# Layer 1 of a two-layer sequence mixer on one core: gates before cells, and five pairs of projections by seven block products

## The chip, the cores and the metric

One core of one Trainium2 chip runs the whole program. Its engines are TensorE (PE, matmuls, with PEld for its weight loads), VectorE (DVE), ScalarE (ACT), GpSimd (POOL) and SyncE (SP, which issues DMAs here). The metric is device microseconds (us) of one execution; lower is better.

## The reference, cut to what matters

x is [512 tokens, 2048] in float32. Layer 0 is an attention layer, which the change leaves as it is. Layer 1 is an mLSTM layer:

```python
proj = x @ w_in                                   # 2048 -> q 1024, k 1024, v 2048, o 2048, gates 16, z 2048
qk = silu(causal_conv4(qk)); q, k = split(qk)     # 8 heads of 128
cell = mlstm(q, k, v, gates)                      # 8 heads of 256, decays from the gates
cell = rmsnorm(cell) * head_norm                  # per head
y = (sigmoid(o) * cell * silu(z)) @ w_out
out = layernorm(ALPHA * x + y)
```

Everything is float32, and the result has to keep close to float32's accuracy.

## The kernel before

**How a product is made.** PE multiplies float32r, a float32 of shorter mantissa. `split` (L166) therefore writes a number as high half plus low half: ACT copies it, rounded, into `hi` (L168), and DVE subtracts to get `lo` (L169). `mm3` (L199) takes three matmuls for a product: hi by hi, hi by lo, lo by hi. The activations of layer 1 (`x1`, 16 k tiles of [128, 512 tokens]) stay in SBUF as pairs. The weights come from HBM in units of 128 partitions by 1024 values: `weights` (L172) loads a unit on SP's queue into one of three `raw` buffers (L181), and `split` turns it into one of three `whi` and three `wlo` buffers.

**Two forms of GEMM.** `gemm_b` (L205) gives [128 columns, 512 tokens] tiles with the weights stationary; a unit is 4 k tiles of 256 columns, 24 matmuls. `gemm_a` (L221) gives [128 tokens, 512 columns] tiles with the activations stationary; a unit is 2 k tiles of 512 columns, 24 matmuls for four token blocks and 12 for two. PSUM has four banks under the name `acc` for these and four under `ps` for everything else.

**Layer 1** is `mlstm` (L798). For each of four pairs of heads it runs a GEMM for the values of both heads (`v_block`, L787), the gate o and z of the first (`gate_out`, L694: two `gemm_b`, Sigmoid on ACT, two multiplies, the last on POOL at L709), q and k of both heads with the causal convolution and SiLU (`conv_silu`, L682), and then o and z of the second head. Each head's cell is a task (`cell`, L725): four steps of q by k with the decays (`decays`, L718, loads them over POOL's queue; L733 is the exponential, L739 the product), then for each of four token blocks the values, a normaliser, a root mean square (L755 to L764, with POOL's power at L255 and a Newton step at L260 to L263), transposes on PE and a multiply into the gate's tile (L773). Values of the first pair are made in two calls, since the second two token blocks of x1 are still being turned when they begin (`Turned`, L846). The gate rows (`gates` and `gate_rows`, L615 and L634) are a task too: a short GEMM and some thirty operations of 8 partitions on DVE.

**What sets the order.** Tasks are generators. `tick` (L116), called between matmuls of a GEMM, runs the next step of a task when a clock that counts matmul columns has come as far as the step's last `yield` asked; in layer 1 one task is under way at a time besides those begun by `start` (L101). `finish` (L125) runs a task to its end at once. That is the order in which instructions are written down; the framework then places each on its engine when, by its own timing, inputs and buffers are free, earlier ones first. Each engine and queue executes in the order so fixed. After layer 1 `out_proj` (L585) multiplies by w_out; its list of inputs (`g1`, L902) calls `finish` on the cell whose head it needs, two k tiles ahead. `resid1` multiplies the residual by layer 0's norm on POOL (L923, L924).

The order of layer 1 in the code before, cut:

```python
for pair in range(H1 // 2):
    ...
    vs = self.v_block(w_in, x, pair, (0, 1, 2, 3))
    gate = self.gate_out(w_in, x, 2 * pair)
    q_ps = self.gemm_b(w_in, 0, pair * 256, x)
    q = [self.conv_silu(q_ps[j], 2 * pair + j) for j in range(2)]
    k_ps = self.gemm_b(w_in, 0, O_K + pair * 256, x)
    k = [self.conv_silu(k_ps[j], 8 + 2 * pair + j) for j in range(2)]
    ...
    for j in range(2):
        hd = 2 * pair + j
        if j:
            gate = self.gate_out(w_in, x, hd)
        cell = self.cell(hd, self.decays(hd), q[j], k[j], vs, gate, gscr if pair < 3 else None)
        t = self.add(cell, 0.0 if j else 4.0)
```

Buffers of SBUF by name, each [128, 512] float32 unless said: `h` 52, `v` 12, `t` 16, `e` 3, `e2` 3 of 256 columns (L41).

Of the kernel before, what the change touches and what calls it, by code (L numbers as in the profile page):

```python
# [40 lines left out]
N_H, N_V, N_T, N_E, N_E2 = 52, 12, 16, 3, 3  # L41
N_RAW, N_HL = 3, 3
# [4 lines left out]
def _pieces(value, bits):  # L47
    """The value as a sum of len(bits) + 1 float32 numbers, the first of so many bits each."""
    out = []
    for b in bits:  # L50
        e = math.floor(math.log2(value)) - b + 1
        p = math.floor(value / 2.0 ** e) * 2.0 ** e
        out.append(p)
        value -= p
    return out + [value]


class Task:
    """Work that is traced between the steps of a GEMM: a generator that yields how many us of TensorE
    time its next step should lie ahead, so that the other engines' work hides behind the GEMM."""  # L60
# [5 lines left out]
class Ahead:  # L66
    """A list whose items are made, in order, some items before they are first asked for."""
# [13 lines left out]
class Kern:  # L81
    def __init__(self, ctx, tc):
# [11 lines left out]
        self.queue, self.active = [], []  # L94

# [64 lines left out]
    def behind(self, ins, after):  # L160
        """Instructions are issued behind earlier ones of their engines."""
# [4 lines left out]
    def split(self, src, hi, lo):  # L166
        """src = hi + lo exactly, hi being src rounded to the float32r mantissa."""
# [3 lines left out]

    def weights(self, src):  # L172
# [3 lines left out]
        raw = self.wp.tile([P, 1024], F32, tag="raw", bufs=N_RAW, name=self.name("raw"))  # L176
        hi = self.wp.tile([P, 1024], F32R, tag="whi", bufs=N_HL, name=self.name("whi"))
        lo = self.wp.tile([P, 1024], F32R, tag="wlo", bufs=N_HL, name=self.name("wlo"))
# [20 lines left out]
    def mm3(self, out, a, b, start, stop):  # L199
        """out += a.T @ b, a and b pairs (hi, lo)."""  # L200
# [4 lines left out]
    def gemm_b(self, w, row0, col0, x, ncol=2, kts=4):  # L205
        """[128 * ncol columns, 512 tokens] as ncol PSUM tiles; x: list of (hi, lo) [128, 512]."""
# [14 lines left out]
    def gemm_a(self, w, col0, x, toks, last=1):  # L221
        """[128 tokens, 512 columns] for tok in toks, a dict of PSUM tiles. The last units of the weights are
        taken token block by token block, so that the first ones are ready early."""
# [3 lines left out]
        for k0 in range(0, nk, 2):  # L227
            src = w[k0 * P : (k0 + 2) * P, col0 : col0 + 512]
            src = src.rearrange("(k p) c -> p k c", p=P)
            if nk - 2 * last <= k0 < nk - 2 * N_HL:  # L230
                raw = self.wp.tile([P, 1024], F32, tag="raw", bufs=N_RAW, name=self.name("raw"))
                raw = raw.rearrange("p (k c) -> p k c", k=2)
# [18 lines left out]
    def rsqrt_small(self, a, w=1):  # L251
        """a ** -0.5 of a [128, w] tile."""
# [5 lines left out]
    def newton(self, y, a, t, eng):  # L258
        """One step for y = a ** -0.5; t is scratch."""
# [6 lines left out]
    # ---------------------------------------------------------------- constants  # L266
# [46 lines left out]
    def rope_tables(self, positions):  # L313
        """cos [128, 512] and sign * sin, row p of frequency p % 32."""
# [30 lines left out]
    def rope(self, src, n, use):  # L345
        """Rotates src (PSUM or SBUF, [n, 512], heads of 64 rows) and hands a float32 tile to use."""
# [55 lines left out]
    def mla(self, x, positions, w_in, w_qb, w_kvb, load_params):  # L402
# [34 lines left out]
        # k_rope: hi and lo of the weights side by side as the stationary operand  # L437
        raw = self.wp.tile([P, 1024], F32, tag="raw", bufs=N_RAW, name="kr_raw")
# [4 lines left out]
        for half in range(2):  # L443
            wt = self.wp.tile([P, 1024], F32R, tag="whi", bufs=N_HL, name=f"kr_w{half}")
# [20 lines left out]
        # the gate path  # L465
# [76 lines left out]
    def attend(self, q, k, qr, kr, vs, g, rot):  # L542
        """g *= softmax(q k) v, transposed."""
# [69 lines left out]
    # ---------------------------------------------------------------- layer 1  # L613

    def gates(self, w_in, x):  # L615
        nc = self.nc
        raw = self.wp.tile([P, 1024], F32, tag="raw", bufs=N_RAW, name="g_raw")
# [3 lines left out]
        for half in range(2):  # L621
            wt = self.wp.tile([P, 1024], F32R, tag="whi", bufs=N_HL, name=f"g_w{half}")
# [11 lines left out]
    def gate_rows(self, ps):  # L634
# [7 lines left out]
        # log_sigmoid(f) = min(f, 0) - log1p(exp(-|f|)), log1p(e) = 2 atanh(e / (2 + e))  # L642
# [35 lines left out]
        gt = self.h()  # L678
        V.tensor_copy(gt[:, 0:256], tp[:, 0:256])
        self.gt = gt[:, 0:256].rearrange("p (s c) -> p s c", c=64)  # L680

    def conv_silu(self, ps, ct):  # L682
        nc, V = self.nc, self.nc.vector
        a, y = self.e(), self.e()
        V.tensor_scalar(a, ps, self.conv_w(3, ct), self.conv_b(ct), ALU.mult, ALU.add)
        for d in range(1, 4):
            V.scalar_tensor_tensor(a[:, d:], ps[:, : SEQ - d], self.conv_w(3 - d, ct), a[:, d:], op0=ALU.mult, op1=ALU.add)
        nc.scalar.activation(y, a, AF.Sigmoid)  # L688
# [36 lines left out]
    def cell(self, hd, d, q, k, vs, gate, gscr):  # L725
# [247 lines left out]
```

## Time and profile before

| | us |
|---|---|
| median of three runs | 1682.35 |
| the three runs | 1682.35, 1682.26, 1683.02 |
| profiled execution, from first to last instruction (its span) | 1679.8 |
| PE busy in it | 1652.9 |
| DVE, ACT, POOL busy | 913.6, 621.1, 205.1 |

The profile gives the span of the execution that it recorded and no other time of it. Busy times are unions over an engine's instructions; matmuls overlap each other, so the mean of one is longer than their spacing. Layer 0 lasts until about 700 us, layer 1 with its output projection from there to the end. [...]

### The profile page before, as it was taken

Reading aid. Unit: us, or ns where it says so; the run is one execution under the profiler, and the core shown is the slowest. Engines: PE = TensorE matmul, PEld = TensorE weight load, DVE = VectorE, ACT = ScalarE, POOL = GpSimd, SP = SyncE. Lnnn points to the kernel's source line nnn. Section 1 sums busy time; section 2 is a strip of 40 time slices with the busy share of each in tenths; the row PEclk is TensorE's granted clock in tenths of the full one; section 3 lists DMA queues with packets and bytes.
Section 4 is the critical chain, followed back from the end, with each engine's and each line's share of the span. In section 5 each row is a group of like instructions: output and inputs, shape, how many; then the busy total and the mean of one; then the engine's idle time right before and its main releaser. Section 6 shows DMA issues by size and latency. Waiting matters only on the chain. (4 is left out here: it accounts for less than half of the span.)

```text
span 1679.8 us, 20372 instructions
## 1 busy us (share of the span) xinstructions
PE 1652.9 (98%) x7706; PEld 1374.3 (82%) x7706; DVE 913.6 (54%) x1750; ACT 621.1 (37%) x952; POOL 205.1 (12%) x262
## 2 busy tenths in 40 slices
PE   8999999999999999999999999999999999999996
PEld 7888888888888888788888888888888888888874
DVE  3374222677778535876564524643365524674476
ACT  3343222454556313454334322432243322542232
POOL 1000000000000000110222101220021101336200
PEclk9999999999999999999999999999999999999998
DMA  7333333322223435674435543434535543366364
GB/s 210 105 97 101 92 97 94 101 63 57 72 74 95 138 100 181 199 233 125 123 104 107 102 97 93 109 105 108 99 110 107 98 101 92 125 201 225 130 203 156
DMA packets 173538, 202.77 MB, mean 121 GB/s; under 512 B 21928, under 2 KB 120328, under 8 KB 173440
## 3 DMA queue, kind: packets, MB, share of 16 engines
q1 hardware_dynamic: 161840, 176.84, 39.1%
q0 software_dynamic: 4688, 12.05, 2.5%
q10 hardware_dynamic: 6912, 12.59, 2.4%
q8 instruction: 60, 0.98, 0.2%
q14 instruction: 38, 0.31, 0.1%
HBM read 187.63 MB, written 11.58 MB: 119 GB/s over the span
## 5 line engine op out<-in xcount | busy, mean ns | idle before, releaser
L196 PE MATMUL acc<-h,whi 128*128 128x512 f32 x2496 | 772.9, 391 | 0.0
L169 DVE TENSOR_TENSOR wlo<-raw,whi 128x1024 fp32r<-128x1024 f32 (+1 forms) x311 | 378.6, 1218 | 508.3 <-ACT whi L168 498.0
L168 ACT CAST whi<-raw 128x1024 fp32r<-128x1024 f32 (+1 forms) x311 | 322.8, 1039 | 644.9 <-PE acc L196 563.5
L196 PEld LDWEIGHTS acc<-h,whi 128*128 128x128 f32 x2496 | 465.4, 188 | 94.7 <-issue 1.0
L196 PE MATMUL acc<-whi,h 128*128 128x512 f32 x1520 | 488.6, 393 | 0.0
L196 PE MATMUL acc<-h,wlo 128*128 128x512 f32 x1248 | 486.4, 390 | 0.0
L196 PEld LDWEIGHTS acc<-whi,h 128*128 128x128 f32 x1520 | 285.3, 188 | 58.1 <-ACT whi L168 0.9
L196 PE MATMUL acc<-wlo,h 128*128 128x512 f32 x760 | 297.2, 391 | 4.8 <-DVE wlo L169 4.8
L196 PEld LDWEIGHTS acc<-h,wlo 128*128 128x128 f32 x1248 | 234.5, 188 | 49.7
L196 PEld LDWEIGHTS acc<-wlo,h 128*128 128x128 f32 x760 | 142.9, 188 | 34.2 <-DVE wlo L169 6.9
L255 POOL TENSOR_TENSOR s<-s,mhalf 128x1 f32<-128x1 f32 x40 | 25.9, 647 | 404.9 <-DVE s L607 153.0
L351 POOL DMA_DIRECT2D e<-e x34 | 17.0, 506 | 411.1 <-DVE e L349 310.7
L196 PE MATMUL ps<-h,h 128*128 128x128 f32 (+3 forms) x288 | 60.7, 319 | 0.0
L562 ACT ACTIVATE t<-ps,s 128x128 f32<-128x128 f32 (+3 forms) x64 | 33.7, 527 | 65.2 <-DVE s L561 65.1
L193 PE MATMUL ps<-ident,t 128*128 128x128 f32 x288 | 47.5, 281 | 6.2 <-DMA t<-in_x_dram 6.0
L196 PEld LDWEIGHTS ps<-h,h 128*128 128x128 f32 x288 | 48.5, 189 | 6.3
L709 POOL TENSOR_TENSOR h<-h,e 128x512 f32<-128x512 f32 x16 | 20.6, 1290 | 261.0 <-DVE e L708 261.0
L193 PEld LDWEIGHTS ps<-ident,t 128*128 128x128 f32 x288 | 37.4, 145 | 17.7 <-issue 3.7
L689 POOL TENSOR_TENSOR e<-e,e 128x512 f32<-128x512 f32 x16 | 29.0, 1815 | 164.6 <-ACT e L688 164.6
L196 PE MATMUL acc<-whi,v 128*128 128x512 f32 x128 | 44.0, 402 | 0.0
L196 PE MATMUL acc<-v,whi 128*128 128x512 f32 x128 | 41.8, 406 | 0.0
L168 ACT CAST h<-e 128x256 fp32r<-128x256 f32 (+1 forms) x48 | 22.8, 478 | 47.3 <-POOL e L689 29.5
(184 smaller groups left out, 1342.2 us busy)
## 6 DMA issues: line engine op xcount, KB each, us to landing
raw<-in_ml_w_in_dram SPq DMA_DIRECT2D x136, 512.0 KB, 5.0
raw<-in_mla_w_out_dram SPq DMA_DIRECT2D x48, 512.0 KB, 4.0
raw<-in_ml_w_out_dram SPq DMA_DIRECT2D x48, 512.0 KB, 4.0
raw<-in_mla_w_in_dram SPq DMA_DIRECT2D x47, 512.0 KB, 3.8
t<-in_x_dram SPq DMA_DIRECT2D x16, 256.0 KB, 6.5
raw<-in_mla_w_kvb_dram SPq DMA_DIRECT2D x16, 256.0 KB, 3.2
raw<-in_mla_w_kvb_dram SPq DMA_DIRECT2D x32, 128.0 KB, 2.4
raw<-in_mla_w_qb_dram SPq DMA_DIRECT2D x32, 128.0 KB, 2.3
```

Source lines behind the costliest of these rows:

```text
L168: a = self.nc.scalar.copy(hi, src)
L169: b = self.nc.vector.tensor_tensor(lo, src, hi.bitcast(F32), op=ALU.subtract)
L193: self.nc.tensor.transpose(out, in_, ident)
L196: self.nc.tensor.matmul(out, lhsT, rhs, start=start, stop=stop)
L255: nc.gpsimd.tensor_tensor(y, a, self.mhalf[:, :w], op=ALU.pow)
L351: nc.gpsimd.dma_start(s[r ^ 32 : (r ^ 32) + 32], b[r : r + 32])
L562: nc.scalar.activation(pt[bi], s[:, :n], AF.Exp, bias=b, scale=scale, accum_out=tot)
L689: nc.gpsimd.tensor_tensor(a, a, y, op=ALU.mult)
L709: nc.gpsimd.tensor_tensor(y, y, t, op=ALU.mult)
```

## The change

Layer 1 is written in another order: all values first, with the gate rows and sums of activations in between, then all gates o and z, then for each pair of heads q, k and the two cells. Values and finished gates go out to DRAM (`vscr`, `ascr`) over POOL's queue and come back over SP's when a pair of heads needs them.

Five stretches, the two middle value blocks together and o and z of each pair of heads, use `quad`. It splits tokens, k tiles (even and odd) and the two column blocks in halves and takes seven products of blocks where eight are plain (Winograd's form). The sums of activation blocks are made once (`mlstm_combos`, kept as pairs in S: 12 `v` and 20 `h` tiles); the sums of weight blocks are made on DVE for each stretch, before they are split.

```diff
+    def combos(self, te, to, alloc):
+        a11, a21, a12, a22 = te[:, 0:256], te[:, 256:512], to[:, 0:256], to[:, 256:512]
+        V.tensor_tensor(a22, a21, a22, op=ALU.subtract)
+        V.tensor_tensor(a21, a11, a21, op=ALU.subtract)
+        V.tensor_tensor(a11, a22, a11, op=ALU.subtract)
+        V.tensor_tensor(a12, a12, a11, op=ALU.add)
...
+            self.split(t, hi, lo)
...
+    def quad(self, w, c0, c1, x, S, done):
...
+        a, b = self.banks
+        self.banks = b, a
...
+        def taken2(t):
+            hi, lo = self.wh(), self.wl()
+            for j in range(2):
+                self.split(t[j], half(hi, j), half(lo, j))
+            return hi, lo
+        def mul(ps, op, j, i, hl):
+            for d in range(2):
+                o = op(i + d)
+                for m in range(2):
+                    s = slice(j * 256 + m * P, j * 256 + (m + 1) * P)
+                    self.mm3(ps[m], (o[0][:, s], o[1][:, s]), (half(hl[0], d), half(hl[1], d)),
+                             i + d == 0, i + d == n - 1)
+                self.tick()
...
+        q1, q5 = two(a), two(a)
+        for i in range(0, n, 2):
+            w11 = raw(0, i, c0)
+            t.append([self.t(), self.t()])
+            for j in range(2):
+                w12 = self.e()
...
+                nc.sync.dma_start(w12, w[kt * P : (kt + 1) * P, c1 : c1 + 512])
+                V.tensor_tensor(t[-1][j], half(w11, j), w12, op=ALU.add)
+            mul(q1, xe, 0, i, taken(w11))
+            mul(q5, so, 1, i, taken2(t[-1]))
+        e1, e5 = two(self.t), two(self.t)
...
+        q7, q6, q3 = two(b), two(a), two(b)
+        for i in range(0, n, 2):
+            w22, w12 = raw(1, i, c1), raw(0, i, c1)
+            V.tensor_tensor(w12, w12, w22, op=ALU.add)
+            for j in range(2):
+                V.tensor_tensor(t[i // 2][j], t[i // 2][j], half(w22, j), op=ALU.add)
+            mul(q7, se, 1, i, taken(w12))
+            mul(q6, se, 0, i, taken2(t[i // 2]))
+            mul(q3, so, 0, i, taken(w22))
+        u, c12 = two(self.t), two(self.t)
+        for m in range(2):
+            V.tensor_tensor(u[m], q6[m], e1[m], op=ALU.add)
+        for m in range(2):
+            V.tensor_tensor(e5[m], e5[m], u[m], op=ALU.subtract)
+            V.tensor_tensor(u[m], u[m], q7[m], op=ALU.add)
+            V.tensor_tensor(c12[m], e5[m], q3[m], op=ALU.add)
+            done(m, 1, c12[m])
+            V.tensor_tensor(e5[m], e5[m], q7[m], op=ALU.subtract)
+            done(2 + m, 1, e5[m])
+        q2, q4 = two(a), two(a)
+        for i in range(0, n, 2):
+            w21 = raw(1, i, c0)
+            for j in range(2):
+                V.tensor_tensor(t[i // 2][j], t[i // 2][j], half(w21, j), op=ALU.add)
+            mul(q2, xo, 0, i, taken(w21))
+            mul(q4, xo, 1, i, taken2(t[i // 2]))
+        for c, q, v in ((0, q2, e1), (2, q4, u)):
+            for m in range(2):
+                V.tensor_tensor(v[m], v[m], q[m], op=ALU.add)
+                done(c + m, 0, v[m])
```

Here `raw` loads two even or two odd k tiles of 512 columns into a `raw` buffer, `taken` splits such a unit at once, and `n` is 8. The order in `mlstm` becomes:

```diff
+        self.values_out(w_in, x, 0, (0, 1), vscr)
+        self.values_out(w_in, late, 0, (2, 3), vscr)
+        late.close()
+        S = []
+        combos = self.add(self.mlstm_combos(x, S))
+        rows = self.start(self.gates(w_in, x))
+        self.values_out(w_in, x, 1536, (0, 1, 2, 3), vscr)
+        self.finish(combos)
+        self.quad(w_in, O_V + 512, O_V + 1024, x, S, ...)
+        self.finish(rows)
+        for pair in range(H1 // 2):
...
+            self.quad(w_in, O_O + pair * 512, O_Z + pair * 512, x, S, gate)
```

`gate` applies SiLU to z and Sigmoid to o on ACT, multiplies them on DVE and sends the product out. `mlstm_combos` adds high and low halves of two k tiles into two `e` tiles, forms `combos` of them and yields 8.0, eight times.

In the cells' part, `v_block` loads four value tiles into `e` and splits them; `conv_silu` makes its first tap on ACT (Identity with scale and bias) and ends in ACT's SiLU instead of Sigmoid and a POOL multiply; `cell` loads its gate into two `t` tiles, multiplies by it before the normalisation, makes one power and one Newton step for all four token blocks instead of one each, scales on ACT, and after the transposes ACT writes the result with the head's norm. Per head this replaces the Sigmoid and multiplies of `gate_out` and the eight multiplies of L773:

```diff
-        for tb in range(NTB):
-            values(tb)
-            yield 2.5 if hd < H1 - 1 else 5.0
-            if tb:
-                turn(tb - 1)
-        yield 3.0
+            V.scalar_tensor_tensor(t, hp[:, 0:DV], rd, gate(tb), op0=ALU.mult, op1=ALU.mult)
+            yield 1.5
+        V.tensor_scalar(ss, ss, 1.0 / DV, EPS, ALU.mult, ALU.add)
+        y = self.rsqrt_small(ss, 4)
+        for tb in range(NTB):
+            nc.scalar.activation(t, t, AF.Copy, scale=y[:, tb : tb + 1])
+        yield 6.0
...
+            nc.scalar.activation(out[j], tp, AF.Copy, scale=self.head_norm(2 * hd + j))
-N_H, N_V, N_T, N_E, N_E2 = 52, 12, 16, 3, 3
+N_H, N_V, N_T, N_E, N_E2 = 52, 12, 16, 3, 2
```

The gates of both heads of a pair are made in the first loop over pairs, so the cells of a pair have only the q and k GEMMs of the next pair beside them, and those of heads 6 and 7 the first block of `out_proj`.

## Rows read from the trace of the kernel before

**Rows 1.** The page: each engine's busy us, share of the span, instructions.
```profile
PE 1652.9 (98%) x7706; PEld 1374.3 (82%) x7706; DVE 913.6 (54%) x1750; ACT 621.1 (37%) x952; POOL 205.1 (12%) x262
```
**Rows 2.** By stretch: length, busy PE, PEld, DVE, ACT, POOL (count), clock, DMA, GB/s.
```profile
680.00:700.00 20.00, 20.00 (x99) 16.04 (x98) 16.82 (x31) 8.06 (x14) 4.57 (x8) 1.00 0.80 261
700.00:720.00 20.00, 17.83 (x83) 14.25 (x82) 15.99 (x27) 10.06 (x15) 0.00 (x0) 1.00 0.52 161
720.00:740.00 20.00, 20.00 (x94) 16.28 (x93) 17.24 (x36) 8.38 (x11) 7.69 (x12) 1.00 0.83 258
850.00:950.00 100.00, 100.00 (x484) 83.91 (x484) 56.28 (x150) 37.26 (x62) 22.90 (x33) 1.00 0.47 99
950.00:1050.00 100.00, 100.00 (x443) 82.81 (x442) 34.38 (x35) 28.10 (x32) 6.00 (x4) 1.00 0.47 103
1620.00:1640.00 20.00, 18.69 (x83) 15.16 (x82) 18.68 (x36) 6.31 (x6) 2.02 (x2) 1.00 0.67 224
```
**Rows 3.** Who waited for whom, whole run: us, times, longest.
```profile
PE acc L196 <- DVE wlo L169: 4.8, 4, 1.9
...
PEld acc L196 <- DVE wlo L169: 6.9, 7, 2.1
```
**Rows 4.** Timeline of PE: start, duration; first and last of 48 matmuls.
```profile
828.05 0.39 PE L196 MATMUL acc<-h,wlo 128*128 128x512 f32 x1
...
838.93 0.39 PE L196 MATMUL acc<-h,wlo 128*128 128x512 f32 x1
```
**Rows 5.** Timeline of ACT and DVE, 1486 to 1494 us.
```profile
1490.68 1.05 ACT L168 CAST whi<-raw 128x1024 fp32r<-128x1024 f32 x1 [0.78 <-PE ps L196]
...
1486.94 1.28 DVE L169 TENSOR_TENSOR h<-g_raw,h 128x512 fp32r<-128x512 f32 x2
1488.14 0.68 DVE L169 TENSOR_TENSOR t<-t,t 128x512 fp32r<-128x512 f32 x1
...
1491.76 1.23 DVE L169 TENSOR_TENSOR wlo<-raw,whi 128x1024 fp32r<-128x1024 f32 x1 [1.27 <-ACT whi L168]
1492.90 0.42 DVE L739 SCALAR_TENSOR_TENSOR t<-ps,t 128x256 f32<-128x256 f32 x1
1493.24 1.28 DVE L169 TENSOR_TENSOR h<-g_raw,h 128x512 fp32r<-128x512 f32 x2
```
**Rows 6.** DMA landings (715 to 760 us; whole run), and groups of layer 1.
```profile
raw<-in_ml_w_in_dram SPq DMA_DIRECT2D x15, 512.0 KB, 4.4
...
raw<-in_ml_w_in_dram SPq DMA_DIRECT2D x136, 512.0 KB, 5.0
...
L169 DVE TENSOR_TENSOR t<-t,t 128x512 fp32r<-128x512 f32 (+3 forms) x32 | 20.1, 628 | 11.6 <-ACT t L168 11.6
L739 DVE SCALAR_TENSOR_TENSOR t<-ps,t 128x512 f32<-128x512 f32 (+3 forms) x32 | 15.5, 486 | 7.5 <-PE ps L196 7.5
L733 ACT ACT_TABLE_LOAD x10 | 12.8, 1283 | 0.5 <-issue 0.3
```
**Rows 7.** Gate weights' landing; timeline of DVE, first and last of the gate rows.
```profile
g_raw<-in_ml_w_in_dram SPq DMA_DIRECT2D x1, 128.0 KB, 9.4
...
784.71 0.68 DVE L641 TENSOR_TENSOR e<-acc,e 8x512 f32<-8x512 f32 x1
...
809.07 0.27 DVE L672 TENSOR_TENSOR t<-e,h 8x128 f32<-8x128 f32 x1
```
**Rows 8.** The tail: busy by stretch, head 7's values on DVE, a group.
```profile
1460.00:1480.00 20.00, 20.00 (x92) 16.49 (x91) 15.40 (x25) 9.95 (x15) 15.52 (x10) 1.00 0.45 132
1500.00:1520.00 20.00, 18.47 (x94) 15.13 (x92) 13.78 (x50) 8.06 (x14) 1.85 (x4) 1.00 0.78 252
...
1495.63 0.15 DVE L755 COPY s<-ps 128x1 f32<-128x1 f32 x1
...
1520.12 1.29 DVE L773 SCALAR_TENSOR_TENSOR h<-ps,par,h 128x128 f32<-128x128 f32 x4
...
L169 DVE TENSOR_TENSOR h<-g_raw,h 128x512 fp32r<-128x512 f32 x12 | 10.8, 924 | 4.5 <-ACT h L168 4.5
```

More of the change, by code (lines that the diff above doesn't have):

```diff
@@ L435, in mla @@
         self.rope_tables(positions)
[L438 removed]
+        raw = self.rt()
         nc.sync.dma_start(raw.rearrange("p (k c) -> p k c", c=ROPE),
@@ L443, in mla @@
         for half in range(2):
-            wt = self.wp.tile([P, 1024], F32R, tag="whi", bufs=N_HL, name=f"kr_w{half}")
+            wt = self.wh()
             w3 = wt.rearrange("p (k c) -> p k c", c=P)
@@ L616, in gates @@
         nc = self.nc
-        raw = self.wp.tile([P, 1024], F32, tag="raw", bufs=N_RAW, name="g_raw")
+        raw = self.rt()
         r3 = raw[:, : KT * 16].rearrange("p (k c) -> p k c", c=16)
@@ L621, in gates @@
         for half in range(2):
-            wt = self.wp.tile([P, 1024], F32R, tag="whi", bufs=N_HL, name=f"g_w{half}")
+            wt = self.wh()
             nc.gpsimd.memset(wt.bitcast(F32), 0.0)
@@ L723, in decays, with cell @@
         return d
-    def cell(self, hd, d, q, k, vs, gate, gscr):
+    def cell(self, hd, q, k, vs, ascr, out, gscr):
         nc, V = self.nc, self.nc.vector
+        d = self.decays(hd)
+        a2 = [self.t().rearrange("p (b c) -> p b c", c=DV) for _ in range(2)]
+        for i in range(2):
+            src = ascr[2 * i * P : (2 * i + 2) * P, hd * DV : (hd + 1) * DV]
+            nc.sync.dma_start(a2[i], src.rearrange("(b p) c -> p b c", p=P))
+        gate = lambda tb: a2[tb // 2][:, tb % 2]
+        yield 5.0
         part = self.part
@@ L742, in cell @@
         c0 = (hd % 2) * 258
-        hn = {}
-        def values(tb):
+        hn = [self.t().rearrange("p (b c) -> p b c", c=DV) for _ in range(2)]
+        ss = self.small(4)
+        for tb in range(NTB):
             hp = self.ps()
@@ new lines, in value_out, with v_block @@
+    def value_out(self, tb, c, t, vscr):
+        self.nc.gpsimd.dma_start(vscr[tb * P : (tb + 1) * P, c : c + 512], t)
+    def v_block(self, vscr, pair):
+        res = []
+        for tb in range(NTB):
+            hi, lo = self.v(F32R), self.v(F32R)
+            raw = self.e()
+            self.nc.sync.dma_start(raw, vscr[tb * P : (tb + 1) * P, pair * 512 : pair * 512 + 512])
+            view = lambda a: a.rearrange("p (h c) -> p h c", c=258)
+            self.nc.gpsimd.memset(view(hi.bitcast(F32))[:, :, DV:258], 1.0)
+            self.split(raw.rearrange("p (h c) -> p h c", c=DV), view(hi)[:, :, 0:DV], view(lo)[:, :, 0:DV])
+            res.append((hi, lo))
+        return res
@@ new lines, in mlstm_combos, with gate @@
+    def mlstm_combos(self, x, S):
+        for i in range(KT // 2):
+            te, to = self.e(), self.e()
+            for t, (hi, lo) in ((te, x[2 * i]), (to, x[2 * i + 1])):
+                self.nc.vector.tensor_tensor(t, hi.bitcast(F32), lo.bitcast(F32), op=ALU.add)
+            alloc = (lambda: self.v(F32R)[:, :SEQ]) if i < 3 else (lambda: self.h(F32R))
+            S.append(self.combos(te, to, alloc))
+            yield 8.0
+    def mlstm(self, w_in, x, gscr, late):
+        nc = self.nc
+        vscr = self.dram.tile([SEQ, H1 * DV], F32, name="vscr")
+        ascr = self.dram.tile([SEQ, H1 * DV], F32, name="ascr")
+        self.values_out(w_in, x, 0, (0, 1), vscr)
[6 more added lines that the diff above has]
+        self.finish(combos)
+        self.quad(w_in, O_V + 512, O_V + 1024, x, S,
+                  lambda tb, col, t: self.value_out(tb, 512 + 512 * col, t, vscr))
+        self.finish(rows)
+        for pair in range(H1 // 2):
+            z = {}
+            def gate(tb, col, t):
+                if col:
+                    nc.scalar.activation(t, t, AF.Silu)
+                    z[tb] = t
+                    return
+                nc.scalar.activation(t, t, AF.Sigmoid)
+                nc.vector.tensor_tensor(t, t, z[tb], op=ALU.mult)
+                nc.gpsimd.dma_start(ascr[tb * P : (tb + 1) * P, pair * 512 : pair * 512 + 512], t)
+            self.quad(w_in, O_O + pair * 512, O_Z + pair * 512, x, S, gate)
@@ L800, in mlstm @@
         tasks = []
         for pair in range(H1 // 2):
-            if pair == 0:
-                vs = self.v_block(w_in, x, 0, (0, 1))
-                vs.update(self.v_block(w_in, late, 0, (2, 3)))
-                rows = self.add(self.gates(w_in, x))
-            else:
-                vs = self.v_block(w_in, x, pair, (0, 1, 2, 3))
-            gate = self.gate_out(w_in, x, 2 * pair)
+            vs = self.v_block(vscr, pair)
             q_ps = self.gemm_b(w_in, 0, pair * 256, x)
@@ L812, in mlstm @@
             k = [self.conv_silu(k_ps[j], 8 + 2 * pair + j) for j in range(2)]
-            if pair == 0:
-                self.finish(rows)
             for j in range(2):
                 hd = 2 * pair + j
-                if j:
-                    gate = self.gate_out(w_in, x, hd)
-                cell = self.cell(hd, self.decays(hd), q[j], k[j], vs, gate, gscr if pair < 3 else None)
+                out = [self.h() if hd < H1 - 1 else self.e() for _ in range(2)]
+                cell = self.cell(hd, q[j], k[j], vs, ascr, out, gscr if pair < 3 else None)
                 t = self.add(cell, 0.0 if j else 4.0)
-                tasks.append((t, gate))
+                tasks.append((t, out))
         return tasks
```

124 lines of the change are left out of this document (65 added, 59 removed).

## The prediction, made before the change ran

> **What bounds the kernel now.** I read the page's busy shares first [rows 1]: TensorE (PE) is busy 98% of the span of 1679.8 us, VectorE (DVE) 54%. Then the same by stretch [rows 2]: in 950 to 1050 us, projections of layer 1, PE is busy all 100 us with DVE at 34%. Third, the waits of PE and its weight load [rows 3]: they waited 4.8 and 6.9 us on DVE's low halves of weights in the whole run. So a matmul less is worth its full spacing, as long as DVE, ScalarE (ACT) and the loads still hand over each block of weights in time. The spacing comes from the timeline [rows 4]: the 48 matmuls that start between 828.05 and 838.93 us take 10.88 us, 0.2267 us each.
>
> The profiled execution has only its span, 1679.8 us; the runs' median is 1682.35, so 2.55 us lie around the span. I take these as unchanged.
>
> **The change, part by part.**
>
> *Fewer matmuls.* A stretch is a pair of 512-column projections. Before it costs 2 x 4 x 16 x 3 = 384 matmuls. In `quad` each of the seven block products is 8 k tiles x 2 token blocks x 3 = 48, together 336. Five stretches save 5 x 48 = 240, and 240 x 0.2267 = **54.4 us** [rows 4]. The shapes stay 128x128 by 512. q, k, gates, two of the four value blocks and the cells' matmuls and transposes keep their counts.
>
> *DVE in a stretch.* Costs are start to start, because neighbours overlap: a 1024-column low half at 1491.76 is followed at 1492.90 (1.14 us), two 512-column ones at 1486.94 by 1488.14 (0.60 each), a 256-column one at 1492.90 by 1493.24 (0.34) [rows 5]. `quad` issues 20 of 1024 columns (16 low halves, 4 sums) and 66 of 512 (24 weight sums, 24 low halves, 14 sums of products, 4 gate products): 20 x 1.14 + 66 x 0.60 = 62.4 us beside 336 x 0.2267 = 76.2 us of PE, 82%.
>
> If each instead cost its whole duration (1.23 and 0.68 in the same rows), a stretch would be 20 x 1.23 + 66 x 0.68 = 69.5 us, 91%; the starts 0.60 apart under durations of 0.64 to 0.68 speak against that. [...]
>
> *What 82% costs PE.* Units are now 12 matmuls, 2.72 us, with three sets of halves, so weights can be ready two units, 5.44 us, ahead; in layer 1 before most units were 24. The nearest rows are stretches with units of 12 and a busy DVE: 680 to 700 and 720 to 740 us (84 and 86%) with PE full, but 700 to 720 (80%) with 2.17 us idle and 1620 to 1640 (93%) with 1.31 [rows 2]. So per stretch between nothing and 2.17/20 x 76.2 = 8.3 us. Two places in the code say where it would be. At the end of the second part ten sums of products, 10 x 0.60 = 6.0 us, are ready at once, the first six 2.72 us before PE changes parts: they end about 3.3 us after it, the two low halves of the second unit behind them, the first of them 0.95 us too late. And in the second part the raw buffer of w12 turns once per 8.16 us: landing 4.4 [rows 6], sum 1.14, ACT's high half 1.05, low half 1.14, four handovers of some 0.1, is 8.1, so any queueing on DVE shows; I allow 0.5 us in three of four rounds. With 0.5 at the last part's end that is 3 us per stretch, **15 us** in five (0 to 41). ACT has 40 halves, 12 copies or activations, none wider than the 1.05 us one [rows 5], and two table loads of 1.28 [rows 6]: below 57 us of 76, covered.
>
> *Gate rows and sums of activations (before the first stretch).* New are 8 rounds of `mlstm_combos`: 4 DVE operations of 512 and 4 of 256 columns, 8 x (2.40 + 1.36) = 30.1 us. Gate rows take DVE from 784.71 to 809.34 us, 24.6 with three low halves of 1.14, so 21.2 [rows 7]. With 8 x 1.14 for the last value block and 4 x (1.14 + 4 x 0.60) = 14.2 for the first part of `quad` DVE has 74.6 us where PE has (32 + 192 + 96) x 0.2267 = 72.5. It can't start evenly: gate rows wait for gate weights that took 9.4 us to land [rows 7] and for 7.3 us of matmuls, and the sums share three e buffers with them. Stall from 0 (sums fill the early gap) to 16 (they don't); I take **7 us**.
>
> *q, k and cells by themselves.* Per pair PE has 192 x 0.2267 = 43.5 us and two cells. The first conv tap goes to ACT; the gate products, gate multiplies and three of four Newton steps a head are gone; transposes leave through ACT. DVE gets 8 x 1.14 for weights, 16 x 0.60 for the convs, 2.4 for values [rows 5] and for each cell about 8 (a head's eighth of two groups, 1.9 + 2.5 [rows 6], and an estimate of 3.6 for the small ones): 37 us of PE's 55, 67%, against 56% in 850 to 950 us with PE full [rows 2]. Two of the four v tile pairs also wait for the cells of the pair before. 0 to 10 us (11% of 55 in two pairs), **2** taken, nearer the full rows.
>
> *The tail.* Before, one cell (head 7) ran in the first output block; now heads 6 and 7 do, in a row, and the block's last k tiles need head 7. PE idled 1.53 us of 1500 to 1520 for head 7 [rows 8]. Bounds: nothing more, or the value chain of head 7 bare, 1495.63 to 1520.12 = 24.5 us [rows 8], less the last two units of 24 matmuls, 10.9: 13.6 us. Also the residual multiplies fall on both cells: POOL was busy 15.52 of 20 us there and the 512-column DVE operations with two SBUF inputs averaged 0.92 us [rows 8] instead of 0.68 [rows 5]. I take **4 us**.
>
> *Costed at nothing.* Loads: w12 twice, and values and gates out to DRAM and back, some 10 + 16 MB more; 720 to 740 us moved 258 GB/s with PE full [rows 2], `quad` wants some 150 on average. POOL issues 32 DMAs and drops 32 multiplies. Two e2 buffers for three: the transposes of layer 0's output would wait up to 0.3 us a k tile, 5 us in all, but for 21 us of value matmuls in front. SP's queue holds 72 more loads; a late one waits on a free e or v tile and holds the raw loads behind it, which I leave in the range.
>
> Sum: -54.4 + 15 + 7 + 2 + 4 = -26.4; span 1653.4, time **1656 us**.
>
> **Rivals.**
> 1. *All of it is hidden.* DVE at 82% and the two full windows at 84 and 86% [rows 2] speak for it, the burst of ten sums against. Only about 2 us of stalls in all: 1682.35 - 54.4 + 2 = 1630.
> 2. *DVE's pace eats the saving.* For it: the 80% window with 11% idle [rows 2], and the weight sums, which depend on each other and on loads, so that whole durations (91%) may be what counts. 8.3 us a stretch, 41 in all, plus 13 elsewhere: 1682.35 - 54.4 + 54 = 1682. [...]
> 3. *Slower: the second part runs one round at a time.* Place: w22 and w12 for a round both need a raw buffer of three, and w22's is kept until the third unit's low half. If the next pair is loaded only after that, a round is landing 5.0 [rows 6] + 1.05 + DVE's 5 x 1.14 = 11.8 for 8.16 us; four rounds in five stretches cost 72 us, with 13 elsewhere 1682.35 - 54.4 + 85 = 1713. It decides from 2.1 us of loss a round upward. For it: in layer 1 the landing of 512 KB went from 4.4 to 5.0; against it: a third buffer, and that 640 to 760 us live on the same three at a similar load.
> 4. That PE's work isn't cut can be left out: the counts are in the loops.
>
> **How the numbers follow.** About 0.2%, 3.4 us, is what a measurement can tell here. Main case 0.52 (1640 to 1672), rival 1 0.16 (1626 to 1640), rival 2 0.18 (1672 to 1687; 0.10 of it faster, 0.07 same, 0.01 slower), rival 3 0.14, of which 0.01 ends level. Faster: 0.52 + 0.16 + 0.10 = 0.78; same 0.08; slower 0.14. The range takes the main case, most of rival 1 and rival 2 up to level: 1632 to 1684.
>
> **What would show it.** PE's matmul count falls by 240 to 7466. Right: in the five stretches PE is busy over 93%, DVE 80 to 85%, and PE's waits are on low halves in the 6 us after a part ends. Rival 2: those waits spread over all parts and DVE is over 90%. Rival 3: ACT's high halves wait on loads of w22 and w12, and the second parts last over 40 us instead of 33. Gate rows: PE idles before the first product with summed activations. Tail: PE waits on head 7's output before the first output block ends. My sum is wrong if the stretches are clean but PE still idles elsewhere by over 20 us, above all between q, k and cells.

## The result and the profile after

| | before | after |
|---|---|---|
| median, runs side by side | 1682.68 (4 runs) | 1745.98 (4 runs) |
| lowest and highest | 1682.26, 1683.94 | 1744.94, 1749.04 |
| span of the profiled execution | 1679.8 | 1743.2 |

The ratio is 1.0379 with a 95% interval of 1.0364 to 1.0394: **63 us slower**, where 26 us faster was forecast and 1684 was the end of the range.

The page of the changed kernel, busy times (beside [rows 1]), PE and its clock in 40 slices of 43.6 us:

```profile
PE 1629.5 (93%) x7466; PEld 1338.5 (77%) x7466; DVE 1095.0 (63%) x1880; ACT 742.3 (43%) x1178; POOL 151.2 (9%) x238
...
PE   8999999999999999999599998998899998679996
...
PEclk9999999999999999999799999999999999789999
```

The 240 matmuls are gone (7706 to 7466), and PE is no longer the whole of the time. It falls in three places: a hole in slice 20, a grain of 8s in the slices behind it, a trough near the end. In both holes the clock falls too. By stretch (length, busy PE, PEld, DVE, ACT, POOL, clock, DMA, GB/s):

```profile
820.00:840.00 20.00, 8.70 (x40) 6.62 (x38) 18.46 (x37) 7.56 (x14) 2.19 (x4) 0.85 0.14 52
840.00:860.00 20.00, 11.21 (x36) 8.46 (x37) 17.84 (x30) 7.89 (x12) 0.00 (x0) 0.64 0.53 158
860.00:1260.00 400.00, 371.30 (x1585) 294.46 (x1584) 300.27 (x403) 183.02 (x250) 15.11 (x30) 1.00 0.58 139
1260.00:1460.00 200.00, 200.00 (x954) 168.37 (x953) 114.60 (x203) 101.74 (x165) 17.28 (x40) 1.00 0.56 133
1460.00:1600.00 140.00, 101.08 (x477) 82.11 (x476) 78.93 (x186) 75.68 (x148) 39.91 (x57) 0.85 0.49 148
```

820 to 860 us: little of PE, DVE at 89% and more; this is before the first product with summed activations. 860 to 1260: nearly all of the five stretches, PE short by 29 us although DVE is only 75% busy. 1260 to 1460: q, k and cells, PE full. 1460 to 1600: the tail, PE short by 39, in parts at a low clock. PE's waits in the whole run (us, times, longest), beside [rows 3]:

```profile
PE acc L204 <- DVE wlo L170: 22.2, 22, 2.0
PE ps L204 <- ACT whi L169: 20.1, 1, 20.1
PE ps L201 <- ACT t L878: 16.9, 6, 8.2
PE ps L204 <- DVE wlo L170: 13.5, 17, 2.2
PE acc L204 <- ACT whi L169: 8.6, 3, 8.0
```

One wait of 20.1 us is the hole, 828.7 to 848.8; 39 short ones on low halves, 31 of them in the stretches, are the grain; those on L878 (a cell's output being scaled) and the one of 8.0 us on ACT are in the tail.

**The stretches, one round.** Timeline of DVE, ACT and SP's queue in the second part of the second stretch. L360 is the sum of w12 and w22, L362 the sums t += w22, L170 low halves, L169 high halves, L313 loads:

```profile
957.81 2.55 DVE L170 TENSOR_TENSOR wlo<-raw,whi 128x1024 fp32r<-128x1024 f32 x2
...
959.05 0.37 SPq L313 DMA_DIRECT2D raw<-in_ml_w_in_dram  x1
...
961.94 1.05 ACT L169 CAST whi<-raw 128x1024 fp32r<-128x1024 f32 x1 [1.79 <-PE ps L204]
962.98 1.29 DVE L362 TENSOR_TENSOR t<-t,raw 128x512 f32<-128x512 f32 x2 [1.42 <-DMA raw<-in_ml_w_in_dram]
965.16 1.22 DVE L360 TENSOR_TENSOR raw<-raw,raw 128x1024 f32<-128x1024 f32 x1 [0.89 <-DMA raw<-in_ml_w_in_dram]
966.31 2.56 DVE L170 TENSOR_TENSOR wlo<-raw,whi 128x1024 fp32r<-128x1024 f32 x2
966.55 1.05 ACT L169 CAST whi<-raw 128x1024 fp32r<-128x1024 f32 x1 [3.56 <-DVE raw L360]
```

The high half of w22 is done at 962.99. Its low half is the first of the pair at 966.31: it stands behind the two sums t += w22 and the sum of w12 and w22 of the next round, which wait for loads. Until it is done w22's raw buffer isn't free, and the next load goes out only when the first of such a pair is done (959.05). So DVE waits for a load, which waited for a low half, which waited behind DVE's wait: 8.50 us from pair to pair, where PE needs 36 x 0.2267 = 8.16. The low half could have started 3.3 us earlier (966.31 - 962.99); DVE ran the three sums that stood ahead of it in its order first, and stood idle 1.42 and 0.89 us for their loads.

In the third and the fifth stretch the same loop is longer. Of the third: the first sum of its second part, two of its pairs, and the first sum of its third part (L381, t += w21):

```profile
1027.42 1.22 DVE L360 TENSOR_TENSOR raw<-raw,raw 128x1024 f32<-128x1024 f32 x1 [1.33 <-DMA raw<-in_ml_w_in_dram]
...
1042.44 2.55 DVE L170 TENSOR_TENSOR wlo<-raw,whi 128x1024 fp32r<-128x1024 f32 x2
...
1052.72 2.55 DVE L170 TENSOR_TENSOR wlo<-raw,whi 128x1024 fp32r<-128x1024 f32 x2
...
1069.99 0.69 DVE L381 TENSOR_TENSOR t<-t,raw 128x512 f32<-128x512 f32 x1 [4.41 <-DMA raw<-in_ml_w_in_dram]
```

From pair to pair it is 10.28 us here, and the second part lasts 42.6 us, where its 144 matmuls need 32.6 and the second stretch took 35.8 (944.47 to 980.25). The raw loads took a median of 5.6 us to land in this part and 3.9 in that of the second stretch; why wasn't tested.

**A ledger.** 63.4 us in the span and the 54.4 saved make 118 us to be found. The experiments put 27 at the start of the first stretch, 42 into the stretches behind it and 49 on the order of layer 1, mostly its tail: 118.

### The profile page after: what moved, and what is told of

It is laid out like the page before. It is cut to its first block, busy times and chain, and to the rows that moved or that the text cites. A ratio compares the mean times of both kernels' runs of the same rounds, so it can differ in the third digit from the quotient of the medians.

```text
span 1743.2 us, 20540 instructions
## 1 busy us (share of the span) xinstructions
PE 1629.5 (93%) x7466; PEld 1338.5 (77%) x7466; DVE 1095.0 (63%) x1880; ACT 742.3 (43%) x1178; POOL 151.2 (9%) x238
## 4 chain that ended last, share of the span: by engine, by line
PE 68%; DVE 14%; DMA 12%; ACT 3%; issue 3%; POOL 0%; SPq 0%; DVEq 0%; POOLq 0%; ACTq 0%
PE acc L204 56%; PE ps L204 10%; DMA raw<-in_ml_w_in_dram 8%; DVE wlo L170 5%; PE ps L201 2%; DMA raw<-in_ml_w_out_dram 2%; ACT whi L169 1%; DVE raw L360 1%; DVE t L381 1%; DVE h L170 1%; DMA e<-in_ml_w_in_dram 1%; DVE e L917 0%; DMA e<-vscr 0%; ACT h L169 0%; DVE t L372 0%
## 5 line engine op out<-in xcount | busy, mean ns | idle before, releaser
L170 DVE TENSOR_TENSOR wlo<-raw,whi 128x1024 fp32r<-128x1024 f32 (+1 forms) x311 | 377.3, 1215 | 324.3 <-ACT whi L169 311.0
L169 ACT CAST whi<-raw 128x1024 fp32r<-128x1024 f32 (+1 forms) x315 | 324.3, 1030 | 570.6 <-PE acc L204 376.9
L204 PE MATMUL acc<-whi,h 128*128 128x512 f32 x1656 | 533.3, 396 | 15.2 <-ACT whi L169 8.6
L204 PE MATMUL acc<-h,whi 128*128 128x512 f32 x1536 | 473.7, 393 | 2.5 <-DVE whi L170 2.5
L204 PEld LDWEIGHTS acc<-h,whi 128*128 128x128 f32 x1536 | 286.8, 189 | 60.7 <-DVE whi L170 2.9
L204 PE MATMUL acc<-h,wlo 128*128 128x512 f32 x736 | 287.5, 391 | 0.0
L204 PEld LDWEIGHTS acc<-h,wlo 128*128 128x128 f32 x736 | 138.4, 188 | 29.5
L204 PE MATMUL ps<-whi,h 128*128 128x512 f32 x488 | 156.3, 392 | 0.0
L204 PE MATMUL ps<-wlo,h 128*128 128x512 f32 x244 | 97.1, 398 | 12.6 <-DVE wlo L170 12.6
L204 PEld LDWEIGHTS ps<-whi,h 128*128 128x128 f32 x488 | 92.1, 189 | 19.1
L169 ACT CAST whi<-t 128x512 fp32r<-128x512 f32 x120 | 69.1, 617 | 59.6 <-PE ps L204 34.4
L201 PE MATMUL ps<-ident,t 128*128 128x128 f32 x352 | 60.1, 288 | 22.6 <-ACT t L878 16.9
L170 DVE TENSOR_TENSOR wlo<-t,whi 128x512 fp32r<-128x512 f32 x120 | 77.9, 685 | 1.1 <-ACT whi L169 0.9
L204 PEld LDWEIGHTS ps<-wlo,h 128*128 128x128 f32 x244 | 45.9, 188 | 28.2 <-DVE wlo L170 19.0
L204 PE MATMUL ps<-whi,v 128*128 128x512 f32 x120 | 42.4, 409 | 20.1 <-ACT whi L169 20.1
```

Of the source, the lines that this page charges most:

```text
L169: a = self.nc.scalar.copy(hi, src)
L170: b = self.nc.vector.tensor_tensor(lo, src, hi.bitcast(F32), op=ALU.subtract)
L201: self.nc.tensor.transpose(out, in_, ident)
L204: self.nc.tensor.matmul(out, lhsT, rhs, start=start, stop=stop)
```

## The experiments

Single executions unless a ratio is given; the kernel before gave 1683.77 beside the first four, 1682.77 beside the next four. The four runs of the changed kernel lie within 4.1 us, so a difference of that size says nothing.

### The order alone

```diff
-    def quad(...): seven block products
+    def quad(self, w, c0, c1, x, S, done):
+        for col, c in ((1, c1), (0, c0)):
+            out = self.gemm_a(w, c, x, range(NTB))
...
-        combos = self.add(self.mlstm_combos(x, S))
```

> The changed order with plain products: the five stretches are computed as two projections of 512 columns each, with eight block products; the sums of activations are left out since nothing reads them; values and gates still go through DRAM, and cells, q, k and the output projection are as in the changed kernel. TensorE has before's count of matmuls again. BUNCH (q, k and cells by themselves are too short for eight cells at some 40 us each, so five heads are left at the end: 57 us): the time of before and the tail's loss, 1683 + 57 = 1740, perhaps 5 more for the gate rows. QUAD (the tail is late because of what the seven-product stretches leave behind: their DRAM traffic, t tiles or late gates): 1683 to 1700.

1730.88 us, span 1729.2. Of this kernel by stretch:

```profile
860.00:1260.00 400.00, 400.00 (x1766) 331.45 (x1765) 98.47 (x87) 122.46 (x149) 10.79 (x20) 1.00 0.47 110
...
1460.00:1480.00 20.00, 11.83 (x52) 10.41 (x50) 12.96 (x36) 12.91 (x28) 3.42 (x9) 0.65 0.46 131
...
1480.00:1500.00 20.00, 7.75 (x20) 5.27 (x21) 8.65 (x18) 14.74 (x22) 5.32 (x8) 0.50 0.24 75
```

PE is full where the stretches were and has the same trough at 1460 to 1500. So the order costs 1729.2 - 1679.8 = 49.4 us with no seven-product stretch in the program. BUNCH holds against QUAD; its size was 8 us too high. The order here includes the transfers of values and gates out to DRAM and back and the new code of the cells: this run keeps both, and does not price them apart.

### Shorter steps for the cells

```diff
-        yield 5.0
+        yield 3.0
-            yield 1.5 if sb < 3 else 1.0
+            yield 0.5
-            yield 1.5
+            yield 0.5
-        yield 6.0
+        yield 3.0
```

> The cells' yields are 3.0, 0.5 (eight times) and 3.0 instead of 5.0, 1.5 and 6.0; nothing else. Theory PACE (in the changed kernel a cell took some 40 us beside 27 us of q and k per head, so five heads were left for the end, which costs about 57 us): the cells keep up, PE's idle time after 1460 us goes from about 50 to below 15 us, total 1746 to about 1700. Rival HOLD (cells are late because v and t tiles come free late): the same 40 us a cell and 1746 within 5 us.

1727.05 us, 19 less than the changed kernel. When the eight heads reach their normaliser, in the changed kernel (the first, the fourth and the last of eight) and, in the second fence, the same three here:

```profile
1350.76 0.16 DVE L874 TENSOR_SCALAR s<-s 128x4 f32<-128x4 f32 x1
...
1469.61 0.16 DVE L874 TENSOR_SCALAR s<-s 128x4 f32<-128x4 f32 x1
...
1582.39 0.16 DVE L874 TENSOR_SCALAR s<-s 128x4 f32<-128x4 f32 x1
```

```profile
1349.62 0.16 DVE L874 TENSOR_SCALAR s<-s 128x4 f32<-128x4 f32 x1
...
1434.63 0.16 DVE L874 TENSOR_SCALAR s<-s 128x4 f32<-128x4 f32 x1
...
1564.93 0.16 DVE L874 TENSOR_SCALAR s<-s 128x4 f32<-128x4 f32 x1
```

In the changed kernel a head takes (1469.61 - 1350.76) / 3 = 39.6 us: the code asks for 22.5 us of distance in ten steps, each step comes at the next tick of the GEMM after it is due, and the cell's own matmuls come on top. So PE is full up to 1460 while the cells fall behind, and five of eight end in the tail. With shorter steps a head takes 28.3. From the last sum of the last stretch to the end the run takes 1725.3 - 1278.6 = 446.7 us against 1743.2 - 1271.4 = 471.8, 25 less; ahead of the first stretch, where the code is the same, it lost 5 more. Heads 6 and 7 still follow each other: 1492.44, 1535.21 and 1564.93 for heads 5 to 7. PACE holds against HOLD, but it had 1700: the cells still don't keep up, and PE idles 17.75 us from 1460 to 1600 (38.9 in the changed kernel).

### Sums of activations in other buffers

```diff
-            te, to = self.e(), self.e()
+            te, to = self.t(), self.t()
```

> The sums of activations use two t tiles for two e tiles; nothing else. Theory EBUF (the first stretch's w12 loads wait for e tiles that the sums hold until 844 us, and the sums wait for e tiles that the gate rows hold): PE's idle time and slow clock between 760 and 860 us, together 26 us, fall to about 10, total 1746 to about 1730. Rival DVEWORK (DVE has more work there than PE has cover, wherever the tiles are): 20 us or more stay, total above 1740.

1745.45 us: no gain. PE's longest wait there fell from 20.1 to 8.5 us, with one of 4.2 ahead of it, and the first stretch ended where it did. The sums now run from 812.7 to 844.4 us (804.3 to 844.0 in the changed kernel): it wasn't the e tiles that made them late.

### Gate rows elsewhere

```diff
-        rows = self.start(self.gates(w_in, x))     # ahead of the second value block
         self.values_out(w_in, x, 1536, (0, 1, 2, 3), vscr)
...
+        rows = self.start(self.gates(w_in, x))     # ahead of the first pair's q
         for pair in range(H1 // 2):
```

> The gate rows move from ahead of the second value block to ahead of the first pair's q and k; nothing else changes. CHAIN (in 760 to 860 us the sums of activations stand behind the 21 us of gate rows on VectorE and share three e tiles with them, so TensorE waits 20.1 us once for the first summed activations and then runs at half clock): the loss there falls from 26 to 6 us or less, 1722 to 1728 in all, with the first copies of the first stretch at about 848 us instead of 867.7. SERIAL (the eight rounds of sums, 30 us one after another, are late by themselves): under 8 us gained, 1737 or more. A cost on the other side would be TensorE idle in the first pair's q and k, where VectorE has the gate rows now.

1721.51 us. This kernel where the hole was, columns as above:

```profile
820.00:840.00 20.00, 20.00 (x90) 16.45 (x89) 14.98 (x20) 9.81 (x15) 0.00 (x0) 1.00 0.59 171
840.00:860.00 20.00, 19.98 (x87) 15.99 (x86) 14.40 (x17) 8.43 (x11) 0.00 (x0) 1.00 0.36 105
```

Its groups by line: sums of activations (L917), the copies of a stretch's first product (L353), the last sums of products (L386), each with its shortest, median and longest time in ns and its first and last start:

```profile
L917 DVE TENSOR_TENSOR e<-h,h x16: 674/684/692, 738.0 to 793.7; 128x512 f32<-128x512 f32 x16
...
L353 ACT COPY t<-ps x6: 587/589/590, 833.3 to 1168.6; 128x512 f32<-128x512 f32 x6
...
L386 DVE TENSOR_TENSOR t<-t,ps x12: 677/681/687, 893.0 to 1239.1; 128x512 f32<-128x512 f32 x12
```

The same groups of the changed kernel:

```profile
L917 DVE TENSOR_TENSOR e<-h,h x16: 654/684/686, 804.3 to 844.0; 128x512 f32<-128x512 f32 x16
...
L353 ACT COPY t<-ps x6: 587/588/589, 867.7 to 1203.2; 128x512 f32<-128x512 f32 x6
...
L386 DVE TENSOR_TENSOR t<-t,ps x12: 679/680/682, 925.5 to 1271.4; 128x512 f32<-128x512 f32 x12
```

The hole is closed: with the gate rows gone from their front, the sums run 66 us earlier, from 738.0, beside the value products. The first stretch comes 34.4 us earlier; 32 x 0.2267 = 7.3 of it are the gates' own matmuls, which moved, so the hole cost 27. CHAIN holds against SERIAL. The run takes the gate rows' work away from this place together with their turn on DVE, so it doesn't divide the 27 between the two. The total gained only 24.5, since the 7.3 came back and 3 more between the stretches and the tail.

### Less in the second part, and another order of its products

The second load of w12 and its sum go, so this kernel leaves a term out of its product and is good for its time alone:

```diff
-            w22, w12 = raw(1, i, c1), raw(0, i, c1)
-            V.tensor_tensor(w12, w12, w22, op=ALU.add)
+            w22 = raw(1, i, c1)
-            mul(q7, se, 1, i, taken(w12))
+            mul(q7, se, 1, i, taken(w22))
```

> Leaves out the second load of w12 and its sum with w22: q7 multiplies w22 in its place, split a second time, so two raw loads per round become one and DVE loses four sums of 1024 columns a stretch (4.6 of 62 us). Theory RAW: the second parts, 36 to 39 us in the changed kernel, come down to 33, and the loss in the stretches falls from 34 to below 12 us, total about 1722. Rival RATE: the loss falls by about the share of DVE work left out, 3 to 6 us, total 1740 or more.

1720.41 us, 25.6 less, the 1722 that RAW gave. But DVE has less to do here too, so this alone doesn't show that the raw buffers are the cause. The product with w22 ahead of the one with t:

```diff
-            mul(q6, se, 0, i, taken2(t[i // 2]))
             mul(q3, so, 0, i, taken(w22))
+            mul(q6, se, 0, i, taken2(t[i // 2]))
```

> In the second part of a stretch the product q3 (with w22 itself) comes before q6, so the raw buffer of w22 is free one unit of 2.7 us earlier; same work. Theory RAW (three raw buffers turn too slowly, DVE waits at its head for a load while low halves of landed units stand behind): the stretches' loss of 34 us falls to about 15, total 1746 to about 1727. Rival RATE (DVE's amount of work per stretch is what costs): within 4 us of 1746.

1751.86 us: no gain, where RAW had 1727. The sums of w12 and w22 waited for loads 49.1 us in the stretches instead of 25.7, the sums t += w22 27.3 instead of 46.5: the wait moved from one to the other. The second load of w12 into the idle e tiles:

```diff
-            w22, w12 = raw(1, i, c1), raw(0, i, c1)
-            V.tensor_tensor(w12, w12, w22, op=ALU.add)
+            w22, w12 = raw(1, i, c1), two(self.e)
+            for j in range(2):
+                kt = 2 * (i + j)
+                nc.sync.dma_start(w12[j], w[kt * P : (kt + 1) * P, c1 : c1 + 512])
+                V.tensor_tensor(w12[j], w12[j], half(w22, j), op=ALU.add)
```

> In the second part of a stretch of the changed kernel a round takes 8.5 to 8.7 us on VectorE (low halves of raw tiles start at 957.81, 966.31, 975.02 us) where TensorE needs 36 x 0.2267 = 8.16. Here the second load of w12 goes, as two halves, into the e tiles that lie idle in this part, so that w22 has the three raw buffers to itself; VectorE's work even grows (two operations of 512 columns for one of 1024, 4 x 0.06 us more a stretch, and as much for the low halves). LOADS (the raw buffers: a round is landing 4.7, sum 1.2 and two low halves 2.55 = 8.5 us, so that w12 comes late): the five second parts fall from 38 to about 34 us, 1720 to 1728. RATE (the amount of VectorE's work is the limit, and what the run without the second load of w12 gained was the 5 x 4 x 1.14 = 23 us of sums that it also left out): 1740 to 1750.

1735.86 us: 10 gained, half of what LOADS expected, and outside RATE's range too. Buffers of their own help, but DVE's sums t += w21 and t += w22 still waited 37.1 and 11.4 us for loads. That left the order on DVE.

### Only the order on DVE

```diff
+        def taken3(t): hi and lo, with the low half kept as last[0]
+        def after(ins):
+            if last[0] is not None:
+                self.behind([ins], [last[0]])
-            V.tensor_tensor(w12, w12, w22, op=ALU.add)
+            after(V.tensor_tensor(w12, w12, w22, op=ALU.add))
...
-            mul(q3, so, 0, i, taken(w22))
+            mul(q3, so, 0, i, taken3(w22))
```

with `after` around the sums of t in parts two and three as well.

> Only VectorE's order changes, in parts two and three of a stretch: the sums of a round are kept behind the low half of w22 of the round before. In the changed kernel that low half could start at 962.99 us (its high half is done) and starts at 966.31, behind two sums that wait 1.42 us and one that waits 0.89 us for loads; its raw buffer is free only then, and the next load is issued only then. ORDER: with the low half first the second part falls from 38 to 34 us; 1718 to 1728. RATE: the same work at the same rate, 1740 to 1750.

1723.47 us, with no work and no buffer changed. One round on DVE in this kernel (L371 is the sum of w12 and w22, L373 the sums of t):

```profile
962.74 1.23 DVE L170 TENSOR_TENSOR wlo<-raw,whi 128x1024 fp32r<-128x1024 f32 x1 [1.90 <-ACT whi L169]
963.88 1.22 DVE L371 TENSOR_TENSOR raw<-raw,raw 128x1024 f32<-128x1024 f32 x1
965.01 1.29 DVE L373 TENSOR_TENSOR t<-t,raw 128x512 f32<-128x512 f32 x2
```

DVE's waits for loads in 860 to 1250 us (us, times, longest), of this kernel and then of the changed one:

```profile
DVE raw L371 <- DMA raw<-in_ml_w_in_dram: 12.4, 8, 2.6
DVE t L373 <- DMA raw<-in_ml_w_in_dram: 9.0, 4, 3.2
...
DVE t L392 <- DMA raw<-in_ml_w_in_dram: 1.2, 2, 0.9
```

```profile
DVE t L362 <- DMA raw<-in_ml_w_in_dram: 46.5, 19, 4.1
DVE raw L360 <- DMA raw<-in_ml_w_in_dram: 25.7, 16, 3.1
DVE t L381 <- DMA raw<-in_ml_w_in_dram: 18.3, 5, 4.4
```

Busy times of this kernel over the stretches, and its groups of first copies (L364) and last sums (L397):

```profile
860.00:1260.00 400.00, 392.35 (x1696) 319.34 (x1696) 316.17 (x424) 195.19 (x267) 21.97 (x42) 0.99 0.63 153
```

```profile
L364 ACT COPY t<-ps x6: 585/587/589, 871.6 to 1190.8; 128x512 f32<-128x512 f32 x6
...
L397 DVE TENSOR_TENSOR t<-t,ps x12: 676/680/683, 926.8 to 1250.0; 128x512 f32<-128x512 f32 x12
```

Now the low half comes when its high half is done, and the sums behind it find their loads landed: 90.5 us of waiting for loads became 22.6, and DVE waits for high halves instead. From the first copy to the last sum lie 5 x 336 - 84 = 1596 matmuls, 361.8 us. The changed kernel takes 1271.4 - 867.7 = 403.7, this one 1250.0 - 871.6 = 378.4: 42 us over became 17, the last sums' own time included. Counted off in PE's matmul starts (96, 144 and 96 a stretch), the second parts lost 26.5 us in the changed kernel and 2.0 here, the third parts 6.2 and 1.9, the first parts of stretches two to five 8.4 and 11.9. ORDER holds; DVE is 79% busy beside a PE of 98%, so RATE falls.

### Together

The three edits in one kernel, and then the last two heads' gates by plain products, head 7's behind its k:

```diff
-        for pair in range(H1 // 2):
+        for pair in range(H1 // 2 - 1):                 # stretches of gates
...
+            if pair == 3:
+                self.gate_head(w_in, x, 6, ascr)
             q_ps = self.gemm_b(w_in, 0, pair * 256, x)
...
+                if hd == 7:
+                    self.gate_head(w_in, x, hd, ascr)
```

> Three of the edits together: the cells' shorter steps (-18.9 us alone), gate rows ahead of the first pair's q and k (-24.5), VectorE's sums kept behind the low half of w22 (-22.5). If they lie in three places of the time that don't touch, as the three accounts say: 1746 - 66 = 1680, some 5 less if the tail no longer starts behind a bunch. If they hide one another (the same TensorE idle time counted twice) or the gate rows now fall on a VectorE that the faster cells fill: 1690 to 1705.

**1665.71 us** in four runs (1664.43 to 1666.59), before 1682.87 beside them: ratio 0.9895, 0.9878 to 0.9911. More than the single gains sum to. By place, in spans: ahead of the first stretch 32.1 us gained (first copies at 835.6), in the stretches 26.9 (376.8 us for 403.7), behind them 20.4 (451.4 for 471.8), 79.4 in all. The first copies of the kernels that keep the hole lay anywhere from 864.9 to 873.0, so the single totals carry some 4 us each of that.

> The same three edits, and only four stretches with seven products: the gates of the last two heads are made by plain products, head 6 just ahead of the last pair's q, head 7 behind its k, so that head 6's cell has 43.5 us of products beside it and only head 7's runs in the output projection, as before. It costs 48 matmuls more, 10.9 us, and two transfers a load. BUNCH (what the tail loses is that cells 6 and 7 follow one another there): 25 to 30 us of the tail go, so 12 to 20 us faster than the run of the three edits. If the tail's loss is the output projection's own (its reloads and weights share the raw buffers): 5 to 11 us slower than it.

**1659.26 us** in four runs (1656.62 to 1662.97): ratio 0.9859, 0.9841 to 0.9876. 6.5 less than the three edits, less than expected: with 10.9 us of matmuls more, 17 of the tail went, not 25 to 30. Busy times from the page of this kernel:

```profile
PE 1618.0 (98%) x7514; PEld 1339.7 (81%) x7514; DVE 1051.6 (64%) x1818; ACT 746.6 (45%) x1173; POOL 154.1 (9%) x242
```

PE is back at 98%, as in [rows 1], with 192 matmuls fewer than before. What is left of the tail's loss, and whether the `t` tiles that a cell holds set when the next one starts, wasn't tried.

## Why the prediction was wrong, step by step

- **Fewer matmuls, 54.4 us: right.** 7466 were counted, and the full-clock spacing stayed: with DVE's order fixed, the 12 matmuls that start from 950.09 up to 952.81 take 2.72 us, 0.2267 each.
- **The stretches, 15 us (0 to 41): 42, and the step that failed is the order on DVE.** The sum priced amounts: 82% of DVE, bursts at a part's end, a buffer that turns in 8.1 us with each operation run as soon as its input is there. It took the code's order for DVE's. The framework had put sums that wait for loads ahead of a low half that frees the buffer for these loads. With only that mended the stretches cost 17, and 15 in the kernel of three edits. That this meets the 15 of the sum is luck: most of it (11.9 us) lies in the first parts, which the sum had at nothing, while the second and third parts, which had all of its 3 us a stretch, lost 0.8. PE was 93% busy and DVE 75%, not 80 to 85, because DVE waited; and the short waits on low halves ran through the parts, a sign given for rival 2.
- **Rival 3** had the right place (second part, raw buffers, one round waiting for the other). Its size, 11.8 us a round, came near in two of five stretches: the third and the fifth had rounds of 10.2 to 11.3 us and second parts of 42.3 by PE's matmuls, over the 40 that it gave as its sign. In the other three a round took 8.2 to 9.7, so the second parts lost 26.5 us in all and not 72. ACT's high halves waited on DVE's sum (3.56 us above), and the sum on the load. It got 0.14, with 13 us for everything else, where 76 were.
- **Rival 2** falls: the 91% by whole durations would have shown as a busy DVE, and the run of DVE's order alone has 79% in the stretches with PE at 98%.
- **Gate rows and sums, 7 us (0 to 16): 27.** The bound of 16 was an early gap on DVE that the sums don't fill, and 7 assumed that they fill half of it. They filled none: the gate rows, which themselves waited for their weights and products, stood ahead of them, DVE idled 15.2 us between 764.4 and 782.5, and the sums started at 804.3. Two sizes were off besides: a round of sums took 4.4 to 4.6 us and not 3.76, where its 256-column operations start 0.45 us apart and not 0.34; and the granted clock of 0.50 behind the hole (last section) had no price. How the 27 divide was not measured. The experiment with other tiles had no gain, the one with the gate rows elsewhere had the whole of it. The sign given (PE idles before the first product with summed activations) was seen, 20.1 us of it.
- **q, k and cells, 2 us; the tail, 4 (0 to 13.6): 49 for the order.** The 2 was right as far as PE goes: PE was full from 1260 to 1460. The step that failed is the tail's, which assumed that only heads 6 and 7 were left when q and k ended. The prediction did not divide the cover by the heads: a head takes 39.6 us by the steps of its task, and there are only 4 x 43.5 / 8 = 21.8 us of q and k per head, plus the cell's own matmuls. Five heads fell into the tail. In the code before, the other GEMMs of layer 1 had lain between the cells. Shorter steps gave back 20.4 us behind the stretches in the kernel of three edits and cover for head 6 another 17; which part has the other 12 of the 49 stays open.
- **The last sentence** ("clean stretches but PE idle elsewhere by over 20 us") named a failure with clean stretches. What came was idle time elsewhere, 76 us, and stretches that were not clean either.

## What to carry to other kernels

A queue's order is part of the price: for each instruction that waits on a load, list what stands behind it on its engine, and ask whether that load is waiting for one of these; one such loop cost 25 us here on an engine 75% busy, and a dependency that only fixes the order took it away. When covered work is regrouped, divide the cover by the pieces: here the lag did not show where PE was full, 200 of 200 us up to 1460, it showed in the tail, 38.9 idle of 140. And a long chain that waits (gate rows) goes where nobody behind it is urgent: 24.5 us here.

## What the hardware showed that wasn't expected

The idle time cost a second time, by the granted clock. In the changed kernel PE stood still for 20.09 us; then (start, duration):

```profile
848.79 0.79 PE L204 MATMUL ps<-whi,v 128*128 128x512 f32 x1 [20.09 <-ACT whi L169]
...
850.54 0.63 PE L204 MATMUL ps<-whi,v 128*128 128x512 f32 x1
850.96 0.63 PE L204 MATMUL ps<-wlo,v 128*128 128x512 f32 x1
...
854.50 0.39 PE L204 MATMUL ps<-wlo,v 128*128 128x512 f32 x1
854.72 0.39 PE L204 MATMUL ps<-whi,v 128*128 128x512 f32 x1
```

From 850.54 to 850.96 one matmul takes 0.42 us instead of 0.2267; at 854.50 to 854.72 the spacing is 0.22 again. The nine matmuls that start from 850.54 up to 854.50 take 3.96 us, where 9 x 0.2267 = 2.04. The granted clock is 0.50 over 848.70 to 854.45, 0.64 over 840 to 860, and 0.50 over the whole of 1480 to 1500 in the run of the order alone, where PE had 7.75 us of work in short pieces. In the run with the gate rows elsewhere, where PE was busy 39.98 of the 40 us from 820 to 860, it is 1.00 in both halves. In the kernel before it falls below 0.9 only in the last of 40 slices, where PE is 60 to 70% busy:

```profile
PE   8999999999999999999999999999999999999996
...
PEclk9999999999999999999999999999999999999998
```

How long PE has to stand still before the clock falls was not measured.
